# A two-batch encoder layer on one core: RMSNorm weights along rows, batch 1's operand sums in pieces, and four FFN tiles that begin with batch 0

## The chip, the cores and the metric

The kernel runs on one core of a Trainium2 chip. The metric is the device time of one execution in microseconds (us), the median of three runs. Beside the runs there is one profiled execution, whose trace gives the rows below. Engines go by short names: PE (TensorE), DVE (VectorE), ACT (ScalarE), POOL (GpSimd), and SP (SyncE), whose queue issues the transfers between HBM and SBUF.

## The reference

One layer of an encoder is applied with the same weights to two requests, here called batch 0 and batch 1, of 512 tokens by 1024 features each, all in float32. The change lies in the second half of the layer: the end of the mixing stage, the second RMSNorm, and the convolutional feed-forward network (FFN) with D_FF = 3072.

```python
def _rmsnorm(x, g):
    xf = x.astype(jnp.float32)
    y = xf * lax.rsqrt(jnp.mean(xf * xf, axis=-1, keepdims=True) + EPS)
    return (y * g.astype(jnp.float32)).astype(x.dtype)

def _layer(x, ...):
    ...
    x = x + (g_a * a_out + g_b * b_out) @ w_o
    xn2 = _rmsnorm(x, norm2_g)
    up = xn2 @ w_up
    gate, val = jnp.split(up, 2, axis=-1)
    gate = _dwconv(gate, ffn_conv_w, ffn_conv_b)
    x = x + (jax.nn.gelu(gate) * val) @ w_down
    return x
```

## The kernel before

**Precision.** Every large product is made in three passes. Each operand is split into a high half, rounded to the fp32r type, and a low half, the rest; hi·hi, hi·lo and lo·hi are added in one PSUM bank. A weight slab of 128 x 512 is so split by a copy on ACT or DVE (L225, L227) and a subtraction on POOL or DVE (L230); which engine takes the subtraction is the list `lo_eng` (L208, L145, L1260).

**The weight stream.** All weights go through one `Stream` (L64 to L110) with a fixed list of slabs in the order of use. Three counters run along it: `nl` loaded, `ns` split, `nu` taken. A ring of eight split slabs holds them. `take(n)` hands out the next n slabs, `done(ring, n)` frees them, and `adv(n)` (L83) splits up to n further slabs if the ring has a free place; loads run up to three ahead of the splits. An instruction is issued on its engine at the place where Python emits it: the schedule is manual, every engine works in the order of the program, and a split stands on ACT, DVE or POOL exactly where `adv` was called. So the number of split slabs that are not yet used, `ns - nu`, called the lead here, is set by these calls. `limit` is a slab that the stream doesn't go past until it is lifted; before the FFN it stands at the first slab "S2" (L280) and is lifted at L1163.

**The mixing stage.** `mix_tile` (L985) makes a tile of the mixed features for one batch: it loads `tha` and `thb` (`th_load`, L977), multiplies and adds on DVE (L1000 to L1004). At its start SP issues the loads of the first `tha` and `thb` and of batch 0's rows `acc`. `o_group` (L1028) is one projection group: 12 matmuls by w_o into one PSUM bank, and one DVE addition into `acc[t]` (L1041). For batch 0, `norm2_tile` (L1009) normalizes a token tile and `norm2_T` (L1014) transposes it, eight PE transposes in two PSUM tiles, multiplies by the norm weights, which stand along partitions there (`v128`, `gb`, L1022 to L1024), and splits the result into the operands B11 and B21. For batch 1 the last eight projection groups go through the loop at L1147: after the second half of each of the four token tiles `norm2_own` (L1093) stores the tile, squares it on ACT (L1100; the output nobody reads goes to a PSUM tile), has POOL make the factor (L1101, L1102) and DVE scale the tile (L1103). `sums_T` (L1105) transposes the tile (L1110), multiplies by the weights (L1116), and forms on DVE, POOL and ACT the operands of a two-by-two Strassen-Winograd scheme with seven products in place of eight: B22, T1, T2, T3, T4, each split in halves (L1117, L1121). `old("B11", j)` reads batch 0's operands, since the two batches are the two column blocks of the scheme.

**The FFN.** It has 24 tiles of 128 gate columns and their 128 value columns. Each tile takes seven products (`prod`, L1166: four steps of k, three matmuls each at L1173, L1174 and L1175) in the order B11, B21, T2, T1, T3, B22, T4, of which B11 and B21 need batch 0 alone. `batch0(f)` (L1183) makes those two: pa to the row `p1` (L1188), and `g0` as p1 plus pb (L1191). `rest(f, pa)` (L1194) makes the other five, the sums `u2`, `p5`, `g1` (L1203 to L1214), the convolution in two DVE operations per batch behind an ACT operation (L1218 to L1221), one GELU for both batches (L1223), the products with the value rows (L1225 to L1230), and the store of the tile to HBM (L1231). The first `EARLY` = 3 tiles run `batch0` ahead of time; their `rest` starts a fresh bank for T2 and adds `p1` later instead of adding onto pa. `up_load` and `up_split` (L241, L257) load the four blocks of w_up for a tile and add and subtract them on DVE (L259) to the slabs "A11", "A12", "S2", "S1", "S3", "S4", "A22". Between the products of the early tiles stand `sums_f(2)` and `sums_f(3)` (L1234), the sums of token tiles 2 and 3, of which transposes use one PSUM tile of two banks:

```python
    batch0(0)
    sums_f(2)
    batch0(1)
    sums_f(3)
    batch0(2)
    close(cm_st)
    lo_eng[:] = [G]
    for f in range(NF):
        ...
        pa = None if f < EARLY else batch0(f)
        ...
        rest(f, pa)
```

**PSUM.** The pool `ps3` (L956) has two tiles "m" of two banks and four banks "t" for the mixing stage; `ps4` (L1160) has "A", "B" and "C" with two banks each and the two-bank "t" for the FFN, allocated when `ps3` is closed. A new tile waits for whoever last used its banks.

**The down projection.** From the last FFN tile on, pairs of rows are fetched back (`h_fetch`, L1239), split by `h_pair` (L1244; ACT L1250, and L1251 on DVE for the first and POOL for the second row), and multiplied by w_down (L1287 to L1290).

## Time and profile before

| | |
|---|---|
| median of three runs | 2131.91 us (2132.86, 2129.9, 2131.91) |
| the profiled execution, its own time | 2130.6 us |
| its span, from the first to the last instruction | 2128.8 us |
| mean granted clock of PE, as a share of full speed | 0.981 |
| instructions | 26423 |

The span is 1.8 us shorter than the execution's own time, and the execution is 1.3 us below the median. Times inside the trace count from the start of the span.

### The profile page before, as it was taken

What the parts mean: (1) busy time and instruction counts of PE and PEld (TensorE: products, weight loads), DVE (VectorE), ACT (ScalarE), POOL (GpSimd) and SP (SyncE); (2) the same over time, 40 slices, a digit from 0 to 9 for tenths busy, and PEclk for the clock granted to TensorE, in tenths of its full rate; (3) what the DMA queues carried; (4) which work ended last, traced back from release to release, by engine and by line L of the source; (5) the groups of instructions that cost most, each with busy time, mean ns of one, the idle gap of its engine ahead of it and who ended that gap; (6) DMA issues with size and microseconds to landing.
All of it is one profiled execution on the core that took longest, in us unless ns stands there. A gap on an engine that the chain in (4) does not pass through costs nothing.

```text
span 2128.8 us, 26423 instructions
## 1 busy us (share of the span) xinstructions
PE 2030.3 (95%) x9571; PEld 1710.2 (80%) x9571; DVE 1253.8 (59%) x1850; ACT 870.4 (41%) x1495; POOL 741.7 (35%) x626
## 2 busy tenths in 40 slices
PE   8989898999999999999999999769999999999999
PEld 6866676787899999998777888557888888788887
DVE  5599998617862671575563443566545455455555
ACT  4488888612431242135443332234443444411210
POOL 3111111034212421413346454454444554432421
PEclk9999999999999999999999999889999999999999
DMA  4535444411111111103547564312222223352322
GB/s 146 156 99 142 119 122 131 157 45 45 31 41 50 36 51 56 34 16 120 178 143 228 165 194 156 99 59 80 89 79 80 85 84 90 114 200 82 108 90 79
DMA packets 202689, 217.14 MB, mean 102 GB/s; under 512 B 28828, under 2 KB 147134, under 8 KB 202558
## 3 DMA queue, kind: packets, MB, share of 16 engines
q1 hardware_dynamic: 200510, 210.21, 31.9%
q0 software_dynamic: 2048, 5.25, 1.0%
q8 instruction: 75, 1.23, 0.2%
q14 instruction: 56, 0.46, 0.1%
HBM read 160.15 MB, written 50.00 MB: 99 GB/s over the span
## 4 chain that ended last, share of the span: by engine, by line
PE 76%; DVE 12%; ACT 5%; issue 3%; DMA 2%; POOL 1%; SPq 0%; DVEq 0%; ACTq 0%; POOLq 0%
PE ps L807 7%; PE ps L808 6%; PE ps L809 6%; PE ps L151 5%; PE ps L152 5%; PE ps L153 5%; PE psd L1287 4%; PE psd L1289 4%; PE psd L1288 4%; PE pfA L1174 4%; PE pfA L1173 4%; PE pfA L1175 4%; DVE u L486 3%; PE o L728 3%; PE pfC L1174 2%
## 5 line engine op out<-in xcount | busy, mean ns | idle before, releaser
L230 POOL TENSOR_TENSOR lo<-raw,hi 128x512 fp32r<-128x512 f32 (+1 forms) x303 | 394.2, 1315 | 643.2 <-ACT hi L227 607.9
L227 ACT CAST hi<-raw 128x512 fp32r<-128x512 f32 (+1 forms) x352 | 204.7, 605 | 272.4 <-PE psd L1289 152.5
L807 PE MATMUL ps<-hi,xh 128*128 128x512 f32 x576 | 251.3, 436 | 0.0
L808 PE MATMUL ps<-lo,xh 128*128 128x512 f32 x576 | 228.5, 397 | 0.0
L809 PE MATMUL ps<-hi,xl 128*128 128x512 f32 x576 | 228.3, 396 | 0.0
L151 PE MATMUL ps<-xh,hi 128*128 128x512 f32 x544 | 217.9, 400 | 0.3 <-DVE xc L403 0.3
L152 PE MATMUL ps<-xl,hi 128*128 128x512 f32 x544 | 216.2, 397 | 0.0
L153 PE MATMUL ps<-xh,lo 128*128 128x512 f32 x544 | 216.1, 397 | 0.0
L1290 DVE TENSOR_TENSOR accd<-accd,psd 128x512 f32<-128x512 f32 x192 | 130.9, 686 | 115.3 <-PE psd L1289 109.7
L807 PEld LDWEIGHTS ps<-hi,xh 128*128 128x128 f32 x576 | 156.0, 271 | 9.7 <-issue 0.2
L808 PEld LDWEIGHTS ps<-lo,xh 128*128 128x128 f32 x576 | 158.3, 275 | 6.0
L809 PEld LDWEIGHTS ps<-hi,xl 128*128 128x128 f32 x576 | 156.4, 271 | 7.9
L1287 PE MATMUL psd<-hi,hp 128*128 128x512 f32 x384 | 150.1, 391 | 3.4 <-DVE gc L1230 3.4
L1289 PE MATMUL psd<-hi,hp 128*128 128x512 f32 x384 | 149.9, 390 | 0.0
L1288 PE MATMUL psd<-lo,hp 128*128 128x512 f32 x384 | 149.9, 390 | 0.0
L707 ACT ACTIVATE p<-p,nm 128x128 f32<-128x128 f32 (+1 forms) x192 | 81.7, 427 | 146.2 <-DVE nm L705 146.2
L629 DVE TENSOR_REDUCE ss<-sq 128x8 f32<-128x512 f32 x48 | 32.9, 685 | 163.6 <-ACT sq L626 163.6
L1173 PE MATMUL pfA<-T,hi 128*128 128x512 f32 x288 | 113.9, 396 | 12.7 <-ACT T L1121 8.3
L151 PEld LDWEIGHTS ps<-xh,hi 128*128 128x128 f32 x544 | 105.2, 193 | 24.6 <-issue 1.4
L152 PEld LDWEIGHTS ps<-xl,hi 128*128 128x128 f32 x544 | 105.1, 193 | 22.2
L153 PEld LDWEIGHTS ps<-xh,lo 128*128 128x128 f32 x544 | 104.7, 192 | 22.7
L1174 PE MATMUL pfA<-T,hi 128*128 128x512 f32 x288 | 113.8, 395 | 1.4 <-DVE T L1117 1.4
(255 smaller groups left out, 4489.7 us busy)
## 6 DMA issues: line engine op xcount, KB each, us to landing
raw<-in_w_in_dram SPq DMA_DIRECT2D x144, 256.0 KB
raw<-in_w_up_dram SPq DMA_DIRECT2D x54, 256.0 KB
r<-in_w_up_dram SPq DMA_DIRECT2D x48, 256.0 KB
f_d<-gc SPq DMA_DIRECT2D x24, 512.0 KB
raw<-in_w_down_dram SPq DMA_DIRECT2D x48, 256.0 KB
hraw<-f_d SPq DMA_DIRECT2D x24, 512.0 KB
sg_d<-sgt SPq DMA_DIRECT2D x16, 512.0 KB
raw<-in_w_lru_out_dram SPq DMA_DIRECT2D x32, 256.0 KB
```

The source lines that it names most:

```text
L151: PE.matmul(out=ps, lhsT=a, rhs=b, start=(k == 0), stop=False)
L152: PE.matmul(out=ps, lhsT=a, rhs=rl(k), start=False, stop=False)
L153: PE.matmul(out=ps, lhsT=wl(k), rhs=b, start=False, stop=(k == n - 1))
L227: A.copy(out=hi[:, 0:n], in_=r[:, 0:n])
L230: e.tensor_tensor(out=lo[:, 0:n], in0=r[:, 0:n], in1=hi[:, 0:n], op=ALU.subtract)
L807: PE.matmul(out=ps, lhsT=a, rhs=hi, start=(k == 0), stop=False)
L808: PE.matmul(out=ps, lhsT=a, rhs=lo, start=False, stop=False)
L809: PE.matmul(out=ps, lhsT=b, rhs=hi, start=False, stop=(k == KD - 1))
L1174: PE.matmul(out=ps, lhsT=a, rhs=bl[:, k], start=False, stop=False, **kw)
L1287: PE.matmul(out=ps, lhsT=hh[:, i, tl], rhs=w[0], start=(i == 0), stop=False)
L1288: PE.matmul(out=ps, lhsT=hh[:, i, tl], rhs=w[1], start=False, stop=False)
L1289: PE.matmul(out=ps, lhsT=hl[:, i, tl], rhs=w[0], start=False, stop=(i == 1))
```

## The change

- **Norm weights.** `gain2`, a row tile with the 1024 norm weights in each partition, is loaded by a broadcast transfer of 512 KB, once ahead of the mixing stage and once more ahead of batch 1's projection. The scale becomes one DVE operation that multiplies by the factor and by the row (`norm2_scale`, for both batches); the products with `gb` behind the transposes go, and the copies, casts and subtractions there read the transposes from PSUM.
- **Batch 1's norm.** `norm2_own` becomes `own_sums` (store, Square, factor) and `own_scale`. The table `after` says behind which of the eight projection groups each of them, and each piece of the sums, is emitted.
- **Batch 1's sums.** `sums_T` becomes a generator of three pieces. Its first piece has the transposes, two ACT copies (one of them to `t3`) and the chain to T1 and T2; the second the low halves, T3 and the two POOL operations to T4; the third T4's halves. Two of the temporaries lie in the scaled token tile itself, one (`t2`) in `st`.
- **Four tiles begin with batch 0.** `EARLY` is 4. The banks "A" and "B" come from a second PSUM pool, `ps4ab`. Tiles 0 and 1 keep their bank pa from `batch0` to `rest` (so that `p1` needs two rows only); tiles 2 and 3 use a bank "C" for the B11 product and start anew in `rest`. Pieces of the sums of tiles 1, 2 and 3 stand between and inside the `batch0` calls.
- **The stream.** It gets a second bound, `hold`, for the splits alone: it stands where `limit` stood, stays there when `limit` is lifted, so that loads go on and splits don't, and is lifted ahead of the fourth `batch0`.

```diff
@@ class Stream
-        self.limit = len(specs)
+        self.limit = self.hold = len(specs)
...
-            if self.ns == self.limit:
+            if self.ns >= min(self.limit, self.hold):
                 return
...
-    EARLY = 3
+    EARLY = 4
...
-    ws.limit = specs.index(("a", ("up", 0, "S2"), 0))
+    ws.limit = ws.hold = specs.index(("a", ("up", 0, "S2"), 0))
...
+    def norm2_sums(t, junk):
...
+        act(out=junk, in_=acc[t], func=AF.Square, accum_out=ss)
...
+    def norm2_scale(t, dst, rs, gain):
+        V.scalar_tensor_tensor(out=dst, in0=acc[t], scalar=rs, in1=gain, op0=ALU.mult, op1=ALU.mult)
+
+    gain2 = mp.tile([128, D], F32, name="gain2")
+    SP.dma_start(out=gain2, in_=norm2_g[0].partition_broadcast(128))
...
-            gb = v128[:, N2 + kk:N2 + kk + 4].rearrange("p (k o) -> p k o", o=1).to_broadcast([128, 4, 128])
-            tmp = mp.tile([128, 4, 128], F32, tag="x2g", bufs=2, name="x2g")
-            V.tensor_tensor(out=tmp, in0=pst, in1=gb, op=ALU.mult)
-            A.copy(out=h[:, :, tl], in_=tmp)
-            V.tensor_tensor(out=l[:, :, tl], in0=tmp, in1=h[:, :, tl], op=ALU.subtract)
+            A.copy(out=h[:, :, tl], in_=pst)
+            V.tensor_tensor(out=l[:, :, tl], in0=pst, in1=h[:, :, tl], op=ALU.subtract)
...
+        A.copy(out=t3, in_=b12)
+        A.copy(out=hi("B22"), in_=b22)
+        sub(V, t1, b12, hi("B11"))
+        sub(V, t1, t1, lo("B11"))
+        sub(V, t2, b22, t1)
+        A.copy(out=hi("T1"), in_=t1)
+        A.copy(out=hi("T2"), in_=t2)
+        yield
+        sub(V, t3, b22, t3)
+        sub(V, lo("T1"), t1, hi("T1"))
+        sub(V, lo("T2"), t2, hi("T2"))
+        sub(V, lo("B22"), b22, hi("B22"))
+        A.copy(out=hi("T3"), in_=t3)
+        sub(G, t1, hi("B21"), t2)
+        sub(G, t1, t1, lo("B21"), ALU.add)
+        sub(G, lo("T3"), t3, hi("T3"))
+        yield
+        A.copy(out=hi("T4"), in_=t1)
+        sub(G, lo("T4"), t1, hi("T4"))
+        yield
...
+    after = {
+        2: lambda: own_sums(0),
+        3: lambda: (own_sums(1), own_scale(0)),
+        4: lambda: (own_scale(1), sums(0, ps3, "m")),
+        5: lambda: (own_sums(2), sums(0)),
+        6: lambda: (own_scale(2), sums(1, ps3, "m"), sums(0)),
+        7: lambda: (own_sums(3), sums(1), own_scale(3)),
+    }
...
-        if hlf:
-            norm2_own(4 + i)
-        if n in (5, 7):
-            sums_o((n - 5) // 2)
+        if n in after:
+            after[n]()
...
     cm_ps, ps4 = open_pool("ps4", space=PSUM)
+    cm_ps_ab, ps4ab = open_pool("ps4ab", space=PSUM)
...
-    bank = lambda nm: ps4.tile([128, 512], F32, tag=nm, bufs=2, name="pf" + nm)
+    bank = lambda nm: (ps4 if nm == "C" else ps4ab).tile([128, 512], F32, tag=nm, bufs=2, name="pf" + nm)
...
-    batch0(0)
-    sums_f(2)
-    batch0(1)
-    sums_f(3)
-    batch0(2)
+    ws.loads()
+    banks = {}
+    banks[0] = batch0(0, mid=lambda: (sums(2, ps4, "t"), sums(1)))
+    sums(2)
+    banks[1] = batch0(1)
+    sums(2)
+    sums(3, ps4, "t")
+    batch0(2, "C")
+    sums(3)
+    ws.hold = len(specs)
+    lo_eng[:] = [G]
+    batch0(3, "C", lambda: sums(3))
     close(cm_st)
-    lo_eng[:] = [G]
...
-        pa = None if f < EARLY else batch0(f)
+        pa = banks.get(f) if f < EARLY else batch0(f)
```

Three places show what moves. The first is DVE's queue over the last two projection groups of batch 1 and the sums behind them. L1041 (L1054 in the change) is the addition of a projection group, L1103 (L1020) the scale of a token tile, L1116 the product with the weights, L1117 (L1127) a sum, L230 the low half of a weight slab. Before:

```order
L1116 TENSOR_TENSOR b12_11342<-pst_11333,v128_73 128x512
L1116 TENSOR_TENSOR b22_11343<-pst_11333,v128_73 128x512
L1117 TENSOR_TENSOR t_11344<-b12_11342,B11_9902 128x512
L1117 TENSOR_TENSOR t_11344<-t_11344,B11_9903 128x512
L1117 TENSOR_TENSOR b22_11343<-b22_11343,t_11344 128x512
L1117 TENSOR_TENSOR T1_11037<-t_11344,T1_11036 128x4x128
L1117 TENSOR_TENSOR t_11344<-B21_9904,b22_11343 128x512
L1117 TENSOR_TENSOR T2_11035<-b22_11343,T2_11034 128x4x128
L1117 TENSOR_TENSOR t_11344<-t_11344,B21_9905 128x512
L230 TENSOR_TENSOR lo_11368<-raw_11231,hi_11367 128x512
L230 TENSOR_TENSOR lo_11386<-raw_11257,hi_11385 128x512
L1041 TENSOR_TENSOR acc_10718<-acc_10718,pso_11363 128x512
```
And in the change:

```order
L1127 TENSOR_TENSOR T2_11021<-t2_11310,T2_11020 128x4x128
L1127 TENSOR_TENSOR B22_11027<-pst_11301,B22_11026 128x4x128
L230 TENSOR_TENSOR lo_11350<-raw_11219,hi_11349 128x512
L230 TENSOR_TENSOR lo_11368<-raw_11245,hi_11367 128x512
L1054 TENSOR_TENSOR acc_10704<-acc_10704,pso_11345 128x512
L1020 SCALAR_TENSOR_TENSOR acc_10702<-acc_10702,sr0_75,gain2_11033 128x1024
L1127 TENSOR_TENSOR acc_10700<-pst_11384,B11_9904 128x512
L1127 TENSOR_TENSOR acc_10700<-acc_10700,B11_9905 128x512
L1127 TENSOR_TENSOR t2_11393<-pst_11384,acc_10700 128x512
L230 TENSOR_TENSOR lo_11408<-raw_11362,hi_11407 128x512
L230 TENSOR_TENSOR lo_11424<-raw_11380,hi_11423 128x512
L1054 TENSOR_TENSOR acc_10704<-acc_10704,pso_11403 128x512
```
Before, the nine operations of tile 0's sums stand in one row ahead of the last two halves of weights; in the change the first pieces of tiles 0 and 1 stand on both sides of the additions of the last two groups (acc_10704), and their first operands come from PSUM (`pst`).

The second place is ACT's queue around the GELU of an ordinary FFN tile. `gc` is the tile under the convolution, L1218 (L1242) its first step, L1223 (L1247) the GELU, L227 the high half of a weight slab, L1188 (L1210) the copy of the B11 product of the next tile. Before:

```order
L227 CAST hi_13175<-r21_13057 128x512
L1218 ACTIVATE gc_13182<-g0_13100,vff_74 128x512
L1218 ACTIVATE gc_13182<-g1_13105,vff_74 128x512
L1223 ACTIVATE gc_13182<-gc_13182 128x1024
L227 CAST hi_13202<-raw_13055 128x512
L227 CAST hi_13229<-r22_13059 128x512
L1188 COPY p1_13233<-pfA_13215 128x512
```
In the change:

```order
L227 CAST hi_13134<-raw_13079 128x512
L1242 ACTIVATE gc_13139<-g0_13057,vff_74 128x512
L1242 ACTIVATE gc_13139<-g1_13062,vff_74 128x512
L1247 ACTIVATE gc_13139<-gc_13139 128x1024
L227 CAST hi_13163<-raw_13098 128x512
L227 CAST hi_13184<-s2_13160 128x512
L1210 COPY p1_13190<-pfA_13170 128x512
```
And in the change on PE, at the end of the next tile's B11 product and the start of its B21 product:

```order
L1195 MATMUL pfA_13170<-B11_9904,hi_13134 128x512
L1196 MATMUL pfA_13170<-B11_9905,hi_13134 128x512
L1197 MATMUL pfA_13170<-B11_9904,lo_13135 128x512
L1195 MATMUL pfB_13171<-B21_9906,hi_13163 128x512
L1196 MATMUL pfB_13171<-B21_9907,hi_13163 128x512
L1197 MATMUL pfB_13171<-B21_9906,lo_13164 128x512
```
Before, the slab that is cast next behind the GELU, hi_13202, goes to the next tile's product B22 (pfC_13253), the sixth of that tile. In the change it is hi_13163, which goes to the next tile's product B21 (pfB_13171), its second, and the one cast ahead of the convolution, hi_13134, goes to B11, its first.

The third place is SP's queue at the start of the mixing stage. L879 stores attention outputs, L980 loads tha and thb, L967 batch 0's rows. Before:

```order
L879 DMA o_d_66<-cg_9079 128x512
L945 DMA y_d_61<-gl_9217 128x512
L879 DMA o_d_66<-cg_9182 128x512
L980 DMA tha_9264<-sg_d_62 128x512
L980 DMA thb_9266<-sg_d_62 128x512
L967 DMA acc_9268<-in_x_prompt_dram 128x1024
```
In the change:

```order
L879 DMA o_d_66<-cg_9079 128x512
L945 DMA y_d_61<-gl_9217 128x512
L879 DMA o_d_66<-cg_9182 128x512
L1023 DMA gain2_9264<-in_norm2_g_dram 128x1024
L980 DMA tha_9266<-sg_d_62 128x512
L980 DMA thb_9268<-sg_d_62 128x512
```
The broadcast of the norm weights stands ahead of tha and thb.

## Rows read from the trace of the kernel before

**Rows 1.** The page, part 1, and PE in part 2.

```profile
PE 2030.3 (95%) x9571; PEld 1710.2 (80%) x9571; DVE 1253.8 (59%) x1850; ACT 870.4 (41%) x1495; POOL 741.7 (35%) x626
...
PE   8989898999999999999999999769999999999999
```

**Rows 2.** Windows: junction, ordinary tile; columns PE, PEld, DVE, ACT, POOL, clock, DMA, GB/s.

```profile
1353.60:1473.80 120.20, 86.51 (x349) 69.64 (x349) 78.19 (x102) 44.37 (x72) 63.54 (x45) 0.83 0.24 71
1500.00:1519.04 19.04, 19.04 (x86) 15.77 (x85) 9.80 (x13) 7.96 (x14) 9.60 (x8) 1.00 0.28 83
```

**Rows 3.** Waits of PE, with releaser: us, count, longest.

```profile
PE pfA L1173 <- ACT junk L1100: 15.2, 1, 15.2
...
PE pfA L1173 <- ACT T L1121: 8.3, 1, 8.3
...
PE ps L151 <- DVE thb L1001: 3.2, 2, 2.2
```

**Rows 4.** Timeline of PE: start, us, operation; tile 3 reaches T4.

```profile
1473.81 0.39 PE L1173 MATMUL pfA<-T,hi 128*128 128x512 f32 x1
```

**Rows 5.** The chain that ended last: a group of eight transposes.

```profile
1226.69 0.87 PE pst L1021 x8
```

**Rows 6.** Timeline of DVE at the junction.

```profile
1352.38 1.28 DVE L1116 TENSOR_TENSOR b<-pst,v 128x512 f32<-128x512 f32 x2
1353.58 0.68 DVE L1117 TENSOR_TENSOR t<-b,B 128x512 f32<-128x512 f32 x1
...
1358.69 1.63 DVE L1117 TENSOR_TENSOR t<-B,b 128x512 f32<-128x512 f32 x1
```

**Rows 7.** Timeline of POOL at the same time.

```profile
1358.06 1.72 POOL L1117 TENSOR_TENSOR T<-b,T 128x512 fp32r<-128x512 f32 x1 [0.73 <-ACT T L1121]
```

**Rows 8.** Timeline of ACT: a Square and the read of its sum.

```profile
1348.75 1.03 ACT L1100 ACTIVATE junk<-acc 128x1024 f32<-128x1024 f32 x1 [3.62 <-DVE acc L1041]
1349.71 0.19 ACT L1100 ACTIVATION_READ_ACCUMULATOR junk<-acc 128x1 f32 x1
```

**Rows 9.** Timeline of PE: first matmuls of two neighbouring products behind a wait.

```profile
1447.64 0.47 PE L1173 MATMUL pfA<-T,hi 128*128 128x512 f32 x1 [2.22 <-ACT hi L227]
...
1451.95 0.49 PE L1173 MATMUL pfC<-B,hi 128*128 128x512 f32 x1
```

**Rows 10.** Timeline of ACT at the first GELU.

```profile
1426.02 1.28 ACT L1223 ACT_TABLE_LOAD   x1 [2.13 <-DVE gc L1221]
```

**Rows 11.** Timeline of DVE in an ordinary tile.

```profile
1569.21 0.69 DVE L1214 TENSOR_TENSOR g<-u,pfC 128x512 f32<-128x512 f32 x1 [1.96 <-PE pfC L1175]
```

**Rows 12.** Timeline of ACT in the same tile: GELU and next cast.

```profile
1572.89 1.06 ACT L1223 ACTIVATE gc<-gc 128x1024 f32<-128x1024 f32 x1 [2.14 <-DVE gc L1221]
1573.86 0.60 ACT L227 CAST hi<-raw 128x512 fp32r<-128x512 f32 x1
```

**Rows 13.** Timeline of POOL in the same tile.

```profile
1574.54 1.29 POOL L230 TENSOR_TENSOR lo<-raw,hi 128x512 fp32r<-128x512 f32 x1 [7.04 <-ACT hi L227]
```

**Rows 14.** Timeline of PE: first and third matmul of the next B21 product.

```profile
1574.45 0.39 PE L1173 MATMUL pfB<-B,hi 128*128 128x512 f32 x1
...
1574.90 0.39 PE L1175 MATMUL pfB<-B,lo 128*128 128x512 f32 x1
```

**Rows 15.** Timeline of PE: the matmul behind a wait and the next.

```profile
1120.02 0.50 PE L153 MATMUL ps<-oh,lo 128*128 128x512 f32 x1 [1.25 <-POOL lo L230]
1120.36 0.39 PE L151 MATMUL ps<-oh,hi 128*128 128x512 f32 x1
```

**Rows 16.** Windows: two microseconds at the start of the mixing stage.

```profile
1126.00:1128.00 2.00, 2.00 (x10) 1.66 (x9) 0.00 (x0) 0.00 (x0) 0.00 (x0) 1.00 1.02 411
```

**Rows 17.** Timeline of POOL in the last FFN tile.

```profile
1849.49 2.37 POOL L1251 TENSOR_TENSOR hp<-hraw,hp 128x1024 fp32r<-128x1024 f32 x1 [4.60 <-ACT hp L1250]
```

**Rows 18.** Timeline of PE: T3 of the last tile, first down product.

```profile
1850.46 0.50 PE L1173 MATMUL pfA<-T,hi 128*128 128x512 f32 x1 [1.13 <-ACT u L1205]
...
1862.35 0.79 PE L1287 MATMUL psd<-hi,hp 128*128 128x512 f32 x1 [3.43 <-DVE gc L1230]
```

More of the change, by code (lines that the diff above doesn't have):

```diff
@@ L1091, in layer_kernel, with own_sums, own_scale @@
     cm_st, st = open_pool("st", side="right")
-    def norm2_own(t):
-        store_acc(t)
-        junk = ps3.tile([128, D], F32, tag="m", bufs=2, name="junk")
-        sr = srs[0]
-        srs.reverse()
-        ss, rs = sr[:, 0:1], sr[:, 1:2]
-        act(out=junk, in_=acc[t], func=AF.Square, accum_out=ss)
-        G.tensor_scalar(out=ss, in0=ss, scalar1=1.0 / D, scalar2=EPS, op0=ALU.mult, op1=ALU.add)
-        G.tensor_tensor(out=rs, in0=ss, in1=mhalf[:, 0:1], op=ALU.pow)
-        V.tensor_scalar(out=acc[t], in0=acc[t], scalar1=rs, scalar2=None, op0=ALU.mult)
+    gain2 = st.tile([128, D], F32, name="gain2")
+    SP.dma_start(out=gain2, in_=norm2_g[0].partition_broadcast(128))
+    rs_own = {}
+    def own_sums(i):
+        store_acc(4 + i)
+        rs_own[i] = norm2_sums(4 + i, ps3.tile([128, D], F32, tag="m", bufs=2, name="junk"))
+    def own_scale(i):
+        norm2_scale(4 + i, acc[4 + i], rs_own.pop(i), gain2)
     def sums_T(i, pst):
@@ L1133, in sums_T @@
-        tt(V, b22, b22, t, ALU.subtract)
-        lo1()
-        lo2 = put("T2", b22, V)
-        tt(V, t, old("B21", 0), b22, ALU.subtract)
-        lo2()
-        tt(V, t, t, old("B21", 1), ALU.add)
-        put("T4", t, G)()
-    def sums_o(i):
-        sums_T(i, ps3.tile([128, 2, 512], F32, tag="m", bufs=2, name="pst"))
+        v = lambda ap: ap.rearrange("p (k t) -> p k t", t=128)
+        b12, b22, t1, t3 = v(pst[:, 0]), v(pst[:, 1]), v(x_t[:, 0:512]), v(x_t[:, 512:1024])
+        t2 = st.tile([128, 4, 128], F32, tag="t2", bufs=1, name="t2")
@@ new lines, in sums_T, with sums @@
+        sub(V, lo("T2"), t2, hi("T2"))
[8 more added lines that the diff above has]
+        yield
+    pieces = {}
+    def sums(i, pool=None, tag=None):
+        if i not in pieces:
+            pieces[i] = sums_T(i, pool.tile([128, 2, 512], F32, tag=tag, bufs=2 if tag == "m" else 1, name="pst"))
+        next(pieces[i])
@@ L1232, in rest @@
         p1.pop(f)
-    def sums_f(i):
-        sums_T(i, ps4.tile([128, 2, 512], F32, tag="t", bufs=1, name="pst"))
     hraw, hT = {}, {}
```

40 lines of the change are left out of this document (16 added, 24 removed).

## The prediction

> **What bounds the kernel now.** I read the page first: TensorE (PE) is busy 95% of the span, and of its 40 slices only two in the middle fall well below 9 [rows 1]. The windows cut out that place. From 1353.6 us, where the last projection group ends, to 1473.8 us, where tile 3 of the FFN reaches its T4 product, 120.2 us go by with 86.5 us of PE work at 0.83 of the clock, while an ordinary tile is 19.04 us of PE without a gap [rows 2]. An ordinary tile has seven products of 12 matmuls, so a product is 2.72 us and a matmul 0.227. The waits of PE name the cause: 15.2 us for the last Square of the norm, 8.3 us for the casts of batch 1's operand sums [rows 3]. Then I checked that the stretch ends where I say: T4 of tile 3 starts at 1473.81 [rows 4].
>
> What PE must do in it is 27 products, 73.4 us, and three groups of eight transposes at 0.87 [rows 5], 2.6 us: 76.0. So 44.2 us is lost there, and that is the most the change can win. Outside it PE waits little, so every new wait there is a loss.
>
> **The junction (own_sums, own_scale, sums_T in pieces, batch0 four times).** A0, the first FFN product, no longer waits: its PSUM banks held projection groups, and its slab is split ahead of it. It starts 0.87 late, behind transposes pulled forward, at 1354.5, and ends at 1357.2. Next in PE's order stand the transposes of tile 2, whose banks the last Square uses. That Square waits for the last projection sum on DVE. By the 2.72 us cadence the sixth group ends at 1348.2 and the subtraction t3 of tile 0 starts at 1349.3; from there to the last projection sum DVE has 14 instructions in a row, with two weight halves among them that wait for ACT.
>
> Their price: an add that reads PSUM takes 0.64, one from SBUF 0.68, but 1.63 when POOL runs beside it, and POOL then 1.72 [rows 6, 7]. Without such meetings (and with 1.25 for the one scale of 1024, twice a 512, and some 3 us of waits for casts) the sum is done by 1361.5; with six POOL operations met, 0.95 each, by 1367. I take 1364.5, as half of the POOL operations fall on adds from PSUM. Square takes 1.2 [rows 8]. So PE waits from 1357.2 to about 1365.8: 8.6 us (5.7 to 11).
>
> After a wait the clock is low: behind one of 2.2 us the next 12 matmuls took 4.31 instead of 2.72 [rows 9]. I add 2 (1.6 to 2.4). T2 of tile 0 then waits for the low half of its slab, which POOL makes behind three operations of tile 3's sums: 3 us (2 to 4). From tile 0 to 1, the slab behind the GELU is late by the 1.1 us worked out below, by the table load of 1.28 [rows 10], by four weight sums that DVE now does ahead of g1 (0.5 to 1.8), and the clock falls once more: 4.5 (3 to 6). From 1 to 2 and 2 to 3 it is 2.25 each (1.6 to 2.9). Together 22.6 us (15.5 to 29). The junction wins 44.2 - 22.6 = **21.6 us** (15 to 28.7).
>
> [...]
>
> **The stream's lead (hold, EARLY = 4).** This is the price that the diff hides. Before, each finished product splits one slab, six ahead of its use. With `hold`, six products free slabs and split none, so when the hold is lifted two split slabs are left; after that one is split for one used, and the lead stays two through the whole FFN. The slab split behind the GELU is now the one of the second product after T4, where before it was that of the fifth or sixth.
>
> In an ordinary tile: g1 starts at 1569.21 [rows 11], the GELU runs 1572.89 to 1573.95, the next high half is cast until 1574.46 [rows 12], POOL makes the low half from 1574.54 to 1575.83 [rows 13]. The second product after T4 starts at 1574.45, and its third matmul, the first that reads the low half, at 1574.90 [rows 14]. With a hand-over of 0.08 (1574.46 to 1574.54) it starts at 1575.91, 1.01 late, and a PE that was stopped takes 0.34 to its next matmul instead of 0.23 [rows 15]: **1.12 us a tile**. Nothing absorbs it: PE has no slack, and the chain from g1 hangs on PE itself, so it comes again in each tile. Tiles 3 to 22 hand over to a tile of this form: 20 x 1.12 = **22.4 us** lost. Bounds: 20, if hand-over and restart shrink by a tenth each; 28, if POOL each time waits out 0.3 us of DVE's product of the GELU, which now comes behind two weight sums.
>
> **The gain row.** 512 KB is loaded on SP's queue ahead of the first tha. Around 1127 the DMA engines are full, at 411 GB/s [rows 16], and PE waits twice, 3.2 us, for what DVE makes of tha and thb [rows 3]. 512 KB at that rate is 1.3 us: I take **1.3** (0 if the waits swallow it, 1.7 with the issue). The second copy of gain2 meets half-idle engines and a PE that is full: 0. Batch 0's norm (POOL's scale moved to DVE, a product less per transpose) lies under full PE and has four PSUM banks in hand: 0; without that cover it would be some 2 us.
>
> **The end of the FFN.** In the last tile ACT casts the first h pair. The low half for T3 now stands on POOL behind that pair's 2.37 us, which starts at 1849.49 [rows 17]: done at 1853.2, needed at 1850.9, in a tile that waited 1.1 there already [rows 18]: +1.2. The first down product waited 3.4 us for a PSUM bank [rows 18]; its bank is free now, but three of four w_down slabs are split behind the last GELU, about the same wait. I take **+1.3** (-1 to 3).
>
> **The sum.** -21.6 + 22.4 + 1.3 + 1.3 = +3.4 us (-9.7 to +17.7). The profiled execution took 2130.6; that makes 2134.0. The median of the three runs is 1.3 above it: **2135.3 us**. A measurement of this kernel can tell about 0.2%, 4.3 us, so the forecast is no change or a little slower.
>
> **Rivals.**
> - The lead costs nothing (place: the second product after T4; it decides when the low half is ready before that product's third matmul, which asks the chain of g1, GELU and casts to be 1 us shorter). Against it: all of its times stand in the rows. For it: an order on ACT that I misread. 2135.3 - 22.4 = 2112.9. 12%.
> - The junction packs well: few meetings of DVE and POOL, a win near 28.7. 2135.3 - 7 = 2128. 14%.
> - The junction does not empty: the change does not do what it says, because each piece still ends in a chain over DVE, ACT and POOL, and the waits only move behind transposes. Price: a win of 10. 2147. 18%.
> - The short wait in each tile pulls the clock down each time. Price: the 1.6 us of rows 9 in 20 tiles, 32 us: 2167. Against it: the wait of 1.25 us in rows 15 was followed by matmuls 0.23 apart. 6%. [...]
>
> **How the numbers follow.** The forecast's own case (2129 to 2142) has 50%. The range is the sum's bounds on the median, 2122 to 2150; it leaves out the first and last rival, 18%. Faster by over 0.2% (below 2127.6): the first rival and a third of the second, 16%. Slower by over 0.2% (above 2136.2): the last two rivals and 22 of the forecast's 50, 46%. Within 0.2%: the rest, 38%.
>
> **What would show it.** In the changed profile: T4 of tile 3 near 1454; a wait of PE of 6 to 11 us at the transposes of tile 2, put down to ACT's Square; in each ordinary tile one wait of PE of about 1 us at the third matmul of pfB, put down to POOL's lo, and a period near 20.16 instead of 19.04 us; a start of the mix stage about 1 us later. A period of 19.04 would make the prediction wrong by the whole 22 us; a T4 of tile 3 later than 1460 or earlier than 1446 would make the junction wrong.

## The result and the profile after

The changed kernel takes 2148.59 us (median of 4 runs, 2144.4 to 2150.14) against 2132.05 before: the ratio is 1.0076, 95% interval 1.0059 to 1.0094. It is slower by 16.5 us; the forecast was 2135.3, slower by 3.4, with a range up to 2150. The profiled execution took 2148.48, 17.9 more than the one before. The page answers to [rows 1], part 1 and PE in part 2:

```profile
PE 2043.2 (95%) x9571; PEld 1707.9 (80%) x9571; DVE 1254.0 (58%) x1833; ACT 872.0 (41%) x1501; POOL 745.8 (35%) x624
...
PE   8989889999999999999999999889999999899999
```

The two low slices in the middle have risen from 7 and 6 to 8 and 8, and an 8 is new in slice 35, at the end of the FFN. PE is busy 13 us longer for the same matmuls; some 10 of these are the 20 ordinary tiles, with 19.52 us busy in each instead of 19.04 (below). Where the 17.9 us went the shares don't tell. I cut both traces at five places that PE's timeline shows in each kernel: its last restart behind POOL's low half in the gate stage (1120.02 before, 1120.07 after), the first projection group, the first transposes of batch 0's norm, the first projection group of batch 1, and T4 of tiles 3 and 23. All times in us, of one profiled execution each:

| stretch | before | after | change | forecast |
|---|---|---|---|---|
| restart to first projection group (gain row) | 63.72 | 65.61 | +1.9 | +1.3 |
| first transposes to batch 1's projection (batch 0's norm) | 82.45 | 90.51 | +8.1 | 0 |
| batch 1's projection to T4 of tile 3 (junction) | 164.83 | 145.76 | -19.1 | -21.6 |
| T4 of tile 3 to T4 of tile 23 (lead; T3 of the last tile) | 382.23 | 406.51 | +24.3 | +22.4 and +1.2 |
| T4 of tile 23 to the end | 272.76 | 275.46 | +2.7 | 0.1 |

The sum is +17.9. The two large terms, junction and lead, came out nearly as forecast; one that I had put at nothing is 8.1. The waits of PE in the changed kernel (columns as in [rows 3]) name the places:

```profile
PE pfB L1197 <- POOL lo L230: 13.5, 20, 0.7
PE pst L1122 <- ACT junk L1014: 9.0, 1, 9.0
...
PE ps L151 <- DVE thb L1001: 4.1, 1, 4.1
PE pst L1037 <- DVE B L1039: 3.5, 1, 3.5
...
PE psd L1314 <- ACT hi L227: 2.5, 1, 2.5
...
PE psd L1315 <- POOL lo L230: 1.6, 1, 1.6
...
PE pst L1037 <- DVE acc L1054: 1.2, 1, 1.2
```

The 15.2 and 8.3 us of [rows 3] are gone; 9.0 stands in their place, at the transposes of tile 2. New are 20 short waits at the third matmul of B21 (L1197 reads the low half), one in each tile from 4 to 23, and two waits at the transposes of batch 0's norm (L1037). The windows of the first stretch, of the norm's stretch, of the junction and of an ordinary tile (columns as in [rows 2]):

```profile
1120.07:1185.68 65.61, 61.51 (x262) 50.30 (x263) 22.32 (x28) 20.12 (x36) 37.93 (x31) 0.97 0.70 222
1228.46:1318.97 90.51, 85.73 (x381) 70.76 (x381) 29.48 (x42) 27.82 (x55) 41.82 (x40) 0.96 0.57 176
1363.53:1464.73 101.20, 83.86 (x346) 66.06 (x344) 61.16 (x78) 40.06 (x66) 58.93 (x42) 0.92 0.28 84
1525.53:1545.72 20.19, 19.52 (x86) 15.61 (x85) 10.18 (x13) 7.97 (x13) 9.81 (x7) 1.00 0.26 79
```

The first two in the kernel before:

```profile
1120.02:1183.74 63.72, 60.49 (x262) 48.97 (x263) 22.65 (x28) 20.14 (x36) 37.92 (x31) 1.00 0.70 220
1226.53:1308.98 82.45, 82.45 (x382) 68.70 (x380) 31.51 (x46) 27.60 (x52) 45.09 (x44) 1.00 0.61 188
```

The junction's window is 101.2 long where [rows 2] had 120.2, at a granted clock of 0.92 instead of 0.83. The tile takes 20.19 instead of 19.04, at a clock of 1.00.

**The ordinary tile.** The timelines of ACT, POOL and PE in one tile of the changed kernel, which answer to [rows 12 to 14]:

```profile
1549.59 1.06 ACT L1247 ACTIVATE gc<-gc 128x1024 f32<-128x1024 f32 x1 [2.14 <-DVE gc L1245]
1550.56 0.60 ACT L227 CAST hi<-raw 128x512 fp32r<-128x512 f32 x1
```

```profile
1551.24 1.34 POOL L230 TENSOR_TENSOR lo<-raw,hi 128x512 fp32r<-128x512 f32 x1 [7.03 <-ACT hi L227]
```

```profile
1551.21 0.50 PE L1195 MATMUL pfB<-B,hi 128*128 128x512 f32 x1
1551.55 0.40 PE L1196 MATMUL pfB<-B,hi 128*128 128x512 f32 x1
1552.63 0.50 PE L1197 MATMUL pfB<-B,lo 128*128 128x512 f32 x1 [0.69 <-POOL lo L230]
1552.97 0.40 PE L1195 MATMUL pfB<-B,hi 128*128 128x512 f32 x1
1553.20 0.39 PE L1196 MATMUL pfB<-B,hi 128*128 128x512 f32 x1
```

The GELU is followed on ACT by the cast of the slab that B21 uses next, POOL makes the low half from 1551.24 to 1552.58, and PE, which was there at 1551.78, starts at 1552.63. That is 0.85; each of the two matmuls that PE had to wait for takes 0.34 to the next instead of 0.23, and the first came 0.05 late itself (the one ahead of it starts at 1550.93): 0.85 + 0.11 + 0.11 + 0.05 are 1.12 of the 1.15. Behind the stop the matmuls are 0.23 apart at once: the granted clock stays at 1.00 (1552.60 to 1555.40).

**Batch 0's norm.** The timelines of DVE, ACT and PE in the changed kernel:

```profile
1228.28 0.68 DVE L1054 TENSOR_TENSOR acc<-acc,pso 128x512 f32<-128x512 f32 x1
1231.10 1.75 DVE L1020 SCALAR_TENSOR_TENSOR x2s<-acc,sr,gain 128x1024 f32<-128x1024 f32 x1 [2.14 <-POOL sr L1016]
1232.77 0.67 DVE L1054 TENSOR_TENSOR acc<-acc,pso 128x512 f32<-128x512 f32 x1
```

```profile
1233.56 1.06 ACT L1014 ACTIVATE x2s<-acc 128x1024 f32<-128x1024 f32 x1 [3.12 <-DVE acc L1054]
```

```profile
1233.50 0.66 PE L1037 MATMUL pst<-ident,x2s 128*128 128x128 f32 x4 [1.24 <-DVE acc L1054]
1237.69 1.09 PE L1037 MATMUL pst<-ident,x2s 128*128 128x128 f32 x4 [3.54 <-DVE B L1039]
```

And POOL and DVE in the kernel before:

```profile
1224.18 1.14 POOL L340 TENSOR_SCALAR x2s<-acc,sr 128x1024 f32<-128x1024 f32 x1
```

```profile
1221.29 0.69 DVE L1041 TENSOR_TENSOR acc<-acc,pso 128x512 f32<-128x512 f32 x1 [2.03 <-PE pso L1037]
1224.00 0.69 DVE L1041 TENSOR_TENSOR acc<-acc,pso 128x512 f32<-128x512 f32 x1 [2.03 <-PE pso L1037]
```

Before, the scale stood on POOL, behind POOL's own factor, and DVE added the projection groups as PE finished them, the first three of these tiles 2.72 us apart. Now the scale stands on DVE and waits 2.14 there for the factor; behind it stands the next tile's projection sum, and its Square waits for that sum. So sum, Square, factor and scale of four tiles have become one chain, of 4.5 to 5.3 us a tile (sums at 1223.22, 1228.28, 1232.77 and 1238.06 by DVE's timeline), and PE runs out of banks: "DVE acc L1054" frees a bank of a projection group. PE's two waits are 4.8 of the 8.1 us. The rest goes with the granted clock, 0.96 over the stretch instead of 1.00: behind the wait of 3.5 us the matmuls stand 0.43 us apart up to 1243.70 instead of 0.23, at a granted clock of 0.50 (1237.69 to 1242.00).

**The junction.** DVE, ACT and PE of the changed kernel around the 9.0 us:

```profile
1370.52 1.60 DVE L230 TENSOR_TENSOR lo<-raw,hi 128x512 fp32r<-128x512 f32 x1 [1.72 <-ACT hi L227]
1373.49 0.95 DVE L230 TENSOR_TENSOR lo<-raw,hi 128x512 fp32r<-128x512 f32 x1 [1.37 <-ACT hi L227]
1374.36 0.67 DVE L1054 TENSOR_TENSOR acc<-acc,pso 128x512 f32<-128x512 f32 x1
```

```profile
1371.93 0.62 ACT L227 CAST hi<-raw 128x512 fp32r<-128x512 f32 x1 [1.45 <-DMA raw<-in_w_up_dram]
...
1375.07 1.03 ACT L1014 ACTIVATE junk<-acc 128x1024 f32<-128x1024 f32 x1 [0.32 <-DVE acc L1054]
```

```profile
1376.27 1.97 PE L1122 MATMUL pst<-ident,acc 128*128 128x128 f32 x8 [9.01 <-ACT junk L1014]
```

The last projection sum stands behind two low halves of weights; DVE waits 3.1 us for their high halves, and ACT, for one of them, for the load of the slab. That is the chain that the forecast described; the loads at its end I had not seen.

Of the 19.1 us that the stretch won, 15.7 lie ahead of the first FFN product: it starts 45.4 us behind batch 1's first projection group (at 1364.38) instead of 61.1 (at 1370.06), and the 15.2 us that it waited before [rows 3] are gone. From there to T4 of tile 3 it is 100.35 instead of 103.75, only 3.4 less.

**The end of the FFN.** POOL and PE of the changed kernel, at T3 of the last tile and at the first down products, which answer to [rows 17, 18]:

```profile
1862.46 2.39 POOL L1272 TENSOR_TENSOR hp<-hraw,hp 128x1024 fp32r<-128x1024 f32 x1 [3.59 <-ACT hp L1271]
1864.81 1.26 POOL L230 TENSOR_TENSOR lo<-r,hi 128x512 fp32r<-128x512 f32 x1
```

```profile
1866.12 0.50 PE L1197 MATMUL pfA<-T,lo 128*128 128x512 f32 x1 [1.95 <-POOL lo L230]
...
1877.25 0.50 PE L1314 MATMUL psd<-hi,hp 128*128 128x512 f32 x1 [2.45 <-ACT hi L227]
...
1879.32 0.79 PE L1315 MATMUL psd<-lo,hp 128*128 128x512 f32 x1 [1.56 <-POOL lo L230]
...
1880.34 0.63 PE L1314 MATMUL psd<-hi,hp 128*128 128x512 f32 x1
1880.76 0.63 PE L1315 MATMUL psd<-lo,hp 128*128 128x512 f32 x1
```

T3's low half stands on POOL behind the h pair, as forecast. The wait for a PSUM bank is gone, but two for w_down slabs have come, and behind them the matmuls are 0.42 apart, at a granted clock of 0.50 (1880.34 to 1884.00).

### The profile page after: what moved, and what is told of

It reads as the page before. It is cut to its first block, busy times and chain, and to the rows that moved or that the text cites. A ratio compares the mean times of both kernels' runs of the same rounds, so it can differ in the third digit from the quotient of the medians.

```text
span 2146.7 us, 26423 instructions
## 1 busy us (share of the span) xinstructions
PE 2043.2 (95%) x9571; PEld 1707.9 (80%) x9571; DVE 1254.0 (58%) x1833; ACT 872.0 (41%) x1501; POOL 745.8 (35%) x624
## 4 chain that ended last, share of the span: by engine, by line
PE 54%; issue 19%; DVE 10%; POOL 10%; ACT 4%; DMA 2%; SPq 0%; POOLq 0%; DVEq 0%; ACTq 0%
POOL lo L230 8%; PE ps L807 7%; PE ps L808 6%; PE ps L809 6%; PE psd L1315 4%; PE psd L1316 4%; PE psd L1314 4%; PE ps L151 4%; PE ps L152 4%; PE ps L153 4%; DVE u L486 3%; PE o L728 3%; PE sp L691 2%; DVE u L478 1%; PE pt L715 1%
## 5 line engine op out<-in xcount | busy, mean ns | idle before, releaser
L230 POOL TENSOR_TENSOR lo<-raw,hi 128x512 fp32r<-128x512 f32 (+1 forms) x302 | 386.0, 1289 | 672.0 <-ACT hi L227 637.0
L227 ACT CAST hi<-raw 128x512 fp32r<-128x512 f32 (+1 forms) x352 | 206.7, 606 | 275.4 <-PE psd L1316 155.7
L1197 PE MATMUL pfA<-T,lo 128*128 128x512 f32 x288 | 112.3, 390 | 3.4 <-POOL lo L230 3.4
L1195 PE MATMUL pfA<-T,hi 128*128 128x512 f32 x288 | 112.3, 390 | 1.3 <-ACT hi L227 1.3
```

The source lines that it names most:

```text
L227: A.copy(out=hi[:, 0:n], in_=r[:, 0:n])
L230: e.tensor_tensor(out=lo[:, 0:n], in0=r[:, 0:n], in1=hi[:, 0:n], op=ALU.subtract)
```

## The experiments

My theory was that the terms of the table are separate mechanisms with the causes just named. Its rivals stand in the expectations. The stretches named below are those of the table.

### Batch 0's scale behind the next tile's sum

```diff
...
-            norm2_tile(i)
+            scale.append(norm2_tile(i))
             store_acc(i)
+            if i >= 1:
+                scale.pop(0)()
...
```

Here `norm2_tile` returns the scale as a function instead of emitting it.

> The changed kernel, with batch 0's scale of a token tile emitted behind the projection sum of the next tile instead of ahead of it. Theory: in the changed kernel the scale on DVE waits 2.1 to 2.2 us for POOL's factor, and the next tile's projection sum is queued behind it, so sum, Square, factor and scale of four tiles form one chain; that cost 8.1 us (the mixing of batch 1's third tile starts 10.0 us later than before, of which 1.9 were there already ahead of the norm). Then PE's waits of 1.24 and 3.54 us at the transposes go, and the time falls by 7 to 8.1 us, to 2140.5 to 2141.5 from 2148.6. Rival: the time goes into the scale itself (1.28 to 2.31 us on DVE instead of 1.13 on POOL) and into copies and subtractions that read PSUM; then the order matters little and the time falls by less than 3 us, to above 2145.6.

Measured: 2141.09, ratio 1.0049 (1.0034 to 1.0064). The norm's stretch is 82.50, that of the kernel before. Both waits at L1037 are gone, though the scale is still on DVE and the copies still read PSUM: the 8.1 us were the order of DVE's queue.

The counterpart is the kernel before with batch 0's norm of the change and nothing else:

```diff
-        rms_tile(mp, acc[t], x_t, G)
...
+        V.scalar_tensor_tensor(out=x_t, in0=acc[t], scalar=rs, in1=gain2, op0=ALU.mult, op1=ALU.mult)
...
```

> The kernel before, with batch 0's norm of the change alone: the row of norm weights (loaded behind the fourth mixing tile), the scale on DVE, copies and subtractions that read PSUM. Theory: the chain of sum, Square, factor and scale on DVE costs 8 us here too, and the rest of the change plays no part in it: 2138 to 2140 from 2131. Rival: the 10 us by which the changed kernel reached batch 1's projection later come from elsewhere (the transfer of the weights, batch 1's order); then less than 3 us.

Measured: 2138.33, ratio 1.0029 (1.0020 to 1.0039). The stretch is 89.30, 6.9 more than before, with waits of 1.2 and 3.5 at the same two places and a granted clock of 0.98. The part by itself makes the kernel before slower.

### The lead

The bound on the splits lifted together with the other:

```diff
-    ws.limit = len(specs)
+    ws.limit = ws.hold = len(specs)
```

> The changed kernel with the second bound of the stream lifted together with the first, so that each product of the FFN splits a slab from the start, as before the change. Theory: the lead goes back to six, the wait of 0.68 us at the third matmul of the B21 product goes in all 20 tiles, and an ordinary tile takes 19.04 us instead of 20.19: 23.0 us less. The end of the FFN (3.9 us) returns by 2 to 4 of it. In the junction the splits stand again between the sums on DVE, ACT and POOL: 0 to 8 us lost there. Together 17 to 27 less, 2122 to 2132. Rival 1: the period of 20.19 comes from the banks or from the fourth early tile, not from the lead; then it stays, and the time is 2146 or more. Rival 2: the bound is what made the junction faster; then T4 of tile 3 moves from 1464.7 to about 1480 and the time is 2135 to 2140.

Measured: 2123.25, ratio 0.9964 (0.9951 to 0.9976). The tile takes 19.04, all 20 waits are gone, and the end is 6.4 us shorter than in the changed kernel (269.02). The junction is 3.2 us longer (148.96): T2 of tile 0 comes 42.1 behind the first product instead of 36.1, T4 of tile 0 another 2.1 later, and 4.9 of that come back in tiles 1 to 3. So the bound does shorten the junction, by 3.2, and costs 23.2 in the tiles and 6.4 at the end. Without it, the way from the first product to T4 of tile 3 takes 103.55, against 103.75 in the kernel before: the 3.4 us won there come with the bound, and the other parts of the change won their 15.7 ahead of the first product.

The bound kept, and the lead caught up:

```diff
         prod(pc, ws.take(1)[0], "T1", True)
+        if f in (3, 4, 5, 6):
+            ws.adv(1)
```

> The changed kernel with its bound on the splits kept, and one more slab split behind the T1 product in each of tiles 3 to 6, so that the lead grows from two to six there. Theory: tiles up to the fifth or so still pay 1.15 us, the others take 19.04 us: 18 to 23 us less, and at the end of the FFN 2 to 4 more, 2122 to 2128. The junction stays as it is (T4 of tile 3 at 1464.7). Rival: four slabs more on DVE, ACT and POOL in these tiles are late themselves and stop PE for 1 us or more each time, or the ring has no free place and the lead stays two: then 2140 to 2150.

Measured: 2117.62, ratio 0.9938 (0.9922 to 0.9954), a larger gain than expected. T4 of PE's timeline in tiles 3, 4 and 5 of this run:

```profile
1462.47 0.39 PE L1195 MATMUL pfA<-T,hi 128*128 128x512 f32 x1
...
1481.51 0.39 PE L1195 MATMUL pfA<-T,hi 128*128 128x512 f32 x1
...
1500.55 0.39 PE L1195 MATMUL pfA<-T,hi 128*128 128x512 f32 x1
```

They are 19.04 apart at once: one slab more, split in tile 3, is enough for the next tile, since the low half that POOL makes behind the GELU is then used a whole product (2.72 us) later. Whether that one slab would do for all the tiles was not tried; the run splits four. The end takes 268.02, 7.4 less than in the changed kernel, because the w_down slabs are split in time again.

The kernel before with a lead of two: `prod` splits nothing in its first four calls.

```diff
+    skip = [4]
...
-            ws.adv(1)
+            if skip[0]:
+                skip[0] -= 1
+            else:
+                ws.adv(1)
```

> The kernel before, in which the first four FFN products split no slab, so that two split slabs are left from there on, as in the changed kernel; nothing else is touched. Theory: the lead alone costs 1.15 us at the B21 product of each tile that has its B21 product in its place (21 tiles, 3 to 23): 24 us; at the end of the FFN some 4 us more, and in the junction 0 to 3 us are won, since four splits less stand between the sums. 2152 to 2162 from 2131. Rival: the period of 20.19 us needs the four early tiles or the banks of the change; then the time stays within 5 us of 2131.

Measured: 2157.43, ratio 1.0113 (1.0096 to 1.0130), a tile of 20.18. Its waits of PE show the same line, in 21 tiles:

```profile
PE pfB L1177 <- POOL lo L230: 14.2, 21, 0.7
```

Banks, early tiles and PSUM reads have no part in it; the lead alone costs 25 us. At the end it shows less here: from T4 of tile 23 it takes 273.4, 0.6 more than before, since PE still waits 3.5 for the PSUM bank there and no w_down slab is late behind that.

### The gain row

The first transfer of the norm weights goes behind the fourth mixing tile:

```diff
-    SP.dma_start(out=gain2, in_=norm2_g[0].partition_broadcast(128))
...
     for c in range(KD):
         mix_tile(0, c)
+        if c == 3:
+            SP.dma_start(out=gain2, in_=norm2_g[0].partition_broadcast(128))
```

> The changed kernel with the first transfer of the norm weights (512 KB) issued behind the fourth mixing tile of batch 0 instead of ahead of the first tha. Theory: the mixing stage starts as before, at 1124.7 instead of 1126.7, and the time falls by 2.0 us (1 to 2.1; before, a wait of 1.07 us stood there that the changed kernel doesn't have), to 2146.5. Rival: the start is set by the stores of the attention outputs, not by this transfer; then nothing changes (2148.6).

Measured: 2148.81, ratio 1.0085 (1.0070 to 1.0100): no gain by the runs. In the trace the first stretch is 64.12, 1.5 less than in the changed kernel, as expected, and the junction 148.80, 3.0 more, most of it between T2 and T4 of tile 0 (15.57 instead of 12.98). In that piece PE waits as long in both kernels (1.3 and 1.4 us), but the granted clock differs. Here and in the changed kernel:

```profile
1401.08:1416.65 15.57, 14.15 (x48) 11.09 (x49) 5.67 (x7) 4.60 (x9) 8.84 (x7) 0.78 0.12 35
```

```profile
1400.51:1413.49 12.98, 11.56 (x48) 8.96 (x49) 5.66 (x7) 4.60 (x9) 8.85 (x7) 1.00 0.14 42
```

So the 2.6 us there go with the clock of that execution. Why it fell behind the same waits in one kernel and not in the other stays open. With the late scale and the catch-up it was tried again, below.

### Both losses undone

The late scale and the catch-up in tiles 3 to 6 together:

> The changed kernel with the late scale of batch 0 and the lead caught up in tiles 3 to 6. Theory: the two losses are independent, one in the mixing stage and one in the FFN, and add: 7.5 and 31 us less than 2148.6, 2110 (2107 to 2113), 1% faster than the kernel before. Rival: one wait takes the place of the other; then 2115 or more.

Measured: 2109.85, ratio 0.9892 (0.9877 to 0.9907). The stretches are 82.48, 145.63, 382.13 and 268.03: each part as in its own run. The junction's 19 us are now won, and the kernel is 1.1% faster than before.

### The junction's wait

Weight halves behind the last sum (the changed kernel, `adv` out of the projection groups):

```diff
-                ws.adv(1)
...
+        if n == 6:
+            ws.adv(4)
         if n in after:
             after[n]()
+        if n == 7:
+            ws.adv(4)
```

> The changed kernel, in which the slabs that the last two projection groups free are split behind the projection sum instead of ahead of it, and those of the last group behind the scale of token tile 3. Theory: the last projection sum stood on DVE behind two halves of weights, which waited for ACT and this for the loads of the slabs, from 1369 to 1374.4; without them the sum, the Square and the transposes of tile 2 come 5 to 7 us earlier, PE's wait of 9.0 us shrinks to 2 to 4, and T4 of tile 3 comes 3 to 7 us earlier against the start of the first product: 2142 to 2146 from 2148.6. Rival 1: DVE, ACT and POOL are full in the junction, and the wait only moves to the T2 product of tile 0: less than 2 us. Rival 2 (the reading of the prediction): the sum was late by meetings of DVE and POOL, not by the halves of weights; then the wait stays above 6 us.

Measured: 2151.17, ratio 1.0085 (1.0070 to 1.0100). The waits of PE:

```profile
PE pst L1121 <- DVE B L1126: 5.1, 1, 5.1
PE pst L1121 <- ACT junk L1014: 5.0, 1, 5.0
```

The wait for the Square shrank from 9.0 to 5.0, a bit short of what I expected, so it did hang on the weight halves; but 5.1 us came up at the transposes of tile 3, which now find their one PSUM tile still read by tile 2's sums. T2 of tile 0 comes 38.8 behind the first product instead of 36.1. That is the first rival: the wait moved, and the junction grew by 4.4 to 150.19 (2.7 ahead of T2, 1.3 between T2 and T4 of tile 0, with a granted clock of 0.87 from 1400.60 to 1413.60 where the changed kernel had 1.00).

The runs from here on are on the kernel with both losses undone. First tile 2's transposes behind the products of the first two FFN tiles:

```diff
-    banks[0] = batch0(0, mid=lambda: (sums(2, ps4, "t"), sums(1)))
-    sums(2)
+    banks[0] = batch0(0, mid=lambda: sums(1))
     banks[1] = batch0(1)
-    sums(2)
+    sums(2, ps4, "t")
+    sums(2)
+    sums(2)
```

> The changed kernel with late scale and caught-up lead (2109.9 us, 1.08% faster than before), in which the transposes of token tile 2 stand behind the products of the first two FFN tiles instead of inside the first, so that PE has three more products to do while the last Square is late. Theory: the junction is bound by the chain of DVE, ACT and POOL that makes the sums and the slab of T2, not by PE; PE's wait of 9.2 us goes from the transposes and comes back at T2 of tile 0, which starts 36 us (35 to 38) behind the first product as now: 2108 to 2112. Rival: PE's own order bounds it; then the 9.2 us are filled, T2 comes 28 us behind the first product, and the time is 2101 to 2103.

Measured: 2114.58, ratio 0.9914 (0.9899 to 0.9929); the junction is 152.47, 6.8 longer than without the edit. PE's waits in its timeline up to T2 of tile 0:

```profile
1366.36 0.77 PE L1200 MATMUL pfA<-B,hi 128*128 128x512 f32 x1 [3.53 <-DVE acc L1055]
...
1381.43 1.94 PE L1127 MATMUL pst<-ident,acc 128*128 128x128 f32 x8 [5.90 <-DVE B L1132]
...
1396.60 0.50 PE L1200 MATMUL pfA<-T,hi 128*128 128x512 f32 x1 [1.26 <-ACT hi L227]
```

The wait didn't go to T2, where I expected it. Part of it stands at the first product of tile 1, whose bank the last projection sum still reads, and part at tile 3's transposes, and T2 came 41.1 behind the first product. Filling PE early puts the sums later on DVE: its first sum of tile 2 starts 21.2 behind the first product instead of 15.6, that of tile 3 29.3 instead of 25.9.

Then the Square's unread output to SBUF:

```diff
...
-        rs_own[i] = norm2_sums(4 + i, ps3.tile([128, D], F32, tag="m", bufs=2, name="junk"))
+        rs_own[i] = norm2_sums(4 + i, x2["T4"][0][:, :, 256:512], True)
```

> The changed kernel with late scale and caught-up lead, in which the Square of batch 1's tiles writes its unread output to SBUF (a part of the T4 operand that is not yet written) instead of PSUM, so that the transposes of tile 2 don't wait for the Square of tile 3. Theory: the transposes start 6 to 7 us earlier, but DVE reads them only behind the scale of tile 3, which stands where it stood; T2 of tile 0 comes 35 to 37 us behind the first product and the time stays within 2 us of 2109.9. Rival: the PSUM banks are the cause of the 9.2 us; then 2101 to 2104.

Measured: 2110.51, ratio 0.9902 (0.9885 to 0.9918). The 9.2 us became waits of 3.6 and 2.9 and smaller ones; T2 comes 37.3 behind the first product, the time is the same. The transposes of tile 2 start 9.4 us earlier, 2.7 behind the first product, but DVE's first sum of tile 2 starts 15.7 behind it (15.6 without the edit) and that of tile 3 25.9, as without it. In three edits PE's wait changed its place and T2 never came earlier, so PE doesn't bound the junction; what DVE, ACT and POOL do in it, with the loads that they wait for, does. Which of these by itself would set the bound was not tried.

### Two small ones on top

The gain row again, now on the kernel with both losses undone:

> The changed kernel with late scale and caught-up lead, and the first transfer of the norm weights behind the fourth mixing tile. Theory: from the last restart of the gate stage to batch 0's first projection group it takes 64.1 us instead of 65.6, as it did in the run with this edit alone, and nothing later takes it back: 2108.3 (2107.5 to 2109). Rival: as in that run, where the time didn't fall, the junction is 2 to 3 us longer at a lower clock; then 2109.5 to 2111.5.

Measured: 2108.39, ratio 0.9883 (0.9868 to 0.9897). The first stretch is 64.34 instead of 65.54, and the junction 145.28 this time. The trace shows 1.2 us won; the interval overlaps that of the kernel without the edit, so the runs don't settle it.

The catch-up in tiles 0 to 3 instead of 3 to 6, on top of that (`if f < 4`):

> The changed kernel with late scale, the later transfer of the norm weights, and the four extra splits in tiles 0 to 3 instead of 3 to 6. Theory: tiles 1 to 3 also stop at a slab that is split late (T1 products: 2.57, 1.19, 1.08 us for the high half and 0.62 each for the low), for the same cause, a lead of two; with a slab more from tile 0 on, from T4 of tile 0 to T4 of tile 3 it takes 46 to 48 us instead of 50.9, and the time falls to 2104 to 2106 from 2108.4. The kernel without the bound took 46.35 us there. Rival: there DVE, ACT and POOL are still behind from the sums, one slab more is late itself, and nothing is won: 2107.5 to 2110.

Measured: 2107.80, ratio 0.9882 (0.9865 to 0.9898): nothing won, the rival. T2 to T4 of tile 0 took 14.9 instead of 13.0, but with the same two waits of PE and a granted clock of 0.89 instead of 1.00, so the 1.9 us aren't shown to come from the edit. From T4 of tile 0 to that of tile 3 it took 49.7 instead of 50.9: the six waits at the T1 products (6.7 us) are gone, but two others at B22 products have come, 3.8 us in tile 1 and 1.6 in tile 3. The timelines of PE and DVE show the first of them, which waits behind a copy of ACT that stands behind the cast of a weight sum, and what the extra splits ran into:

```profile
1422.36 0.58 PE L1201 MATMUL pfC<-B,hi 128*128 128x512 f32 x1 [3.81 <-ACT p L1242]
```

```profile
1403.67 0.69 DVE L259 TENSOR_TENSOR s<-r,r 128x512 f32<-128x512 f32 x1 [8.31 <-DMA r<-in_w_up_dram]
...
1419.70 0.69 DVE L259 TENSOR_TENSOR s<-r,r 128x512 f32<-128x512 f32 x1 [4.46 <-DMA r<-in_w_up_dram]
```

DVE stood 8.3 and 4.5 us for slabs that were not loaded yet. The first of these sums starts 47.5 us behind the first product, and in the run without the edit 47.6: so early in the FFN the loads, not the splits, are late.

## Why the prediction was right where it was, and where not

The direction and the range held; the likeliest time, 2135.3, was 13 us low, and its own case (2129 to 2142) missed. That the range held, by 1.4 us, was luck: its room was reckoned for the junction, the lead, the gain row and the end, and batch 0's norm, the largest miss, had none. The two profiled executions are 17.9 apart, where the sum's upper bound is 17.7.

- **The lead: right.** 22.4 forecast, 23.0 measured (20 tiles of 1.15), at the matmul, the engine and with nearly the period (20.16, measured 20.19) that the order of ACT's queue and [rows 11 to 15] gave. The two runs that give the lead back and the one that takes it from the kernel before settle the cause. The parts came out less well than their sum: the third matmul was 0.85 late where 1.01 was reckoned, and the first one was stopped too, by ACT's cast, which the forecast didn't have (0.05 and a second restart of 0.11). The lower bound of 20 does not follow from the tenth that it names: hand-overs and restart a tenth shorter make 21.9.
- **Batch 0's norm: the step that failed.** "Batch 0's norm (POOL's scale moved to DVE, a product less per transpose) lies under full PE and has four PSUM banks in hand: 0". It cost 8.1. I counted the scale's work on DVE as hidden and didn't ask what is queued behind it there. The trace of before would have told it: from the start of a Square to the end of POOL's factor it takes 2.1 us (1222.01 to 1224.08), so an instruction on DVE that waits for it holds every later projection sum by as much, and each of these releases the next Square. Four banks did not cover a chain of four tiles. Of the 14.5 us between the forecast's sum (+3.4) and the measured one (+17.9), 8.1 are this, 2.6 the end, 2.5 the junction, and 1.3 the lead and the gain row.
- **The junction: right in its mechanism, 2.5 us too good.** 21.6 forecast, 19.1 measured. The wait at tile 2's transposes was 9.0 where 8.6 was reckoned. From the start of T3's subtraction of tile 0 to the last projection sum it was 15.8 us (1359.26 to 1375.03), reckoned at 15.2, and DVE's waits for casts were 3.4 of these, reckoned at 3. Most of the rest is in tile 2 to 3: 4.1 us lost where 2.25 stood, at a granted clock of 0.90; from tile 1 to 2, at 1.00, it was 2.0. The sign that was to show the junction failed all the same: T4 of tile 3 came at 1464.73, later than 1460. It was an absolute time, and 10.0 us had been lost ahead of the junction, in the norm and the gain row; without these it would be 1454.7, where 1454 was forecast.
- **The gain row: right, a bit low.** 1.3 forecast, 1.9 measured, above its bound of 1.7. PE's waits there are 0.9 of it (4.1 for the 3.2 of [rows 3]); the rest goes with the granted clock, 0.97 over the stretch instead of 1.00, which the forecast left out. The run that moves the transfer got back 1.5 in the trace and nothing in its time.
- **The end: low.** T3 of the last tile waits 1.95 as described, and its stretch has 1.3 more than the 23.0 of the tiles (1.2 forecast); but where "about the same wait" was forecast at the first down product, 2.7 us more were measured. PE's waits are 4.0 us there where 3.4 stood before; most of the rest goes with the granted clock, 0.88 over the first 29 us behind T4 of the last tile where it was 0.94 before (with the late scale and the same waits the end is 274.0). It is a second price of the lead: with the lead back the end is 268.0, 4.7 shorter than before, and no wait for a PSUM bank is left; with the lead of two the late slabs and the granted clock of 0.50 behind them take 7.4.
- **The rivals.** The nearest time was that of "the junction does not empty", 2147, but its mechanism was wrong: the junction did empty. That the lead costs nothing and that the clock falls each time were both refuted. In the trace the 20 waits of 0.7 us left the granted clock at 1.00, while behind waits of 9.0 and 3.5 us it did fall (0.92 over the junction, 0.96 over the norm's stretch).
- **Sums that read PSUM: right.** The forecast took 0.64 for an add that reads PSUM and 0.68 for one from SBUF [rows 6]. On DVE's timeline the subtraction from PSUM at 1356.61 and the one from SBUF at 1357.33 take 0.69 each: the read from PSUM took no longer.

## What to carry to other kernels

When an operation moves to another engine, write down what stands behind it in that engine's queue and what it will wait for: an instruction that waits for a short result of a third engine can chain tiles that ran side by side; here that cost 8.1 us, and four spare banks did not cover it. When a stream of prepared operands is held back, look at the lead that is left once it runs again: here it did not come back by itself, and four extra splits, the first of which was enough for the next tile, brought back 24 us in the tiles and 7 at the end. And where PE waits in a stretch that other engines bound, removing its wait may only move it: three edits here did so, and two of them made that stretch longer, by 4.4 and 6.8 us.

## What the runs showed of the hardware

- The part of the program ahead of the restart at 1120 us is the same in all fourteen profiled executions, and reached that point between 1117.4 and 1123.1: a spread of 5.7 us that no edit made. Over that part the granted clock was 0.98 in the kernel before and in the changed one, which reached the point at 1120.02 and 1120.07; over the whole execution it was 0.989 in the earliest of the fourteen (the gain row on the kernel with both losses undone) and 0.981 in the latest (the kernel before with a lead of two). Differences of a few us between two traces are read by stretches, not by spans.
- A DVE operation that reads an operand from PSUM was not lengthened by POOL beside it, one with two SBUF operands was. In the changed kernel the subtraction `acc<-pst,B` at 1366.22 took 0.68 and the next, `acc<-acc,B`, 1.07, both while POOL was at work from 1365.17 to 1367.45. Behind 1110 us in that trace, 136 such operations on two tiles of 128x512, one of them in PSUM, lie beside POOL at work for their whole length and took 0.67 to 0.69 us; those with both tiles in SBUF took up to 1.78.
- The same two waits of PE (1.3 and 1.4 us, at the start of T2 of tile 0) were followed by a granted clock of 1.00 up to T4 in the changed kernel, and of 0.78 in the run with the later transfer.
